# Attention: the causal mask inside the running product, and full steps' running product over pairs of keys

## The chip, the cores and the metric

The kernel runs on one core of a Trainium2 chip. The metric is the device time of one execution in microseconds (us), as the median of several runs. The engines are PE (matrix products; PEld is its loading of weights), DVE (vector), ACT (activation functions), POOL (general vector) and SP (issues DMAs). Each works through its own queue in order; semaphores order them among each other.

## The reference

One decoder block on a sequence of 2048 tokens with 1024 channels, all in float32. What matters here is the attention with 8 heads of 64 channels:

```python
def stick_breaking_attention(q, k, v):
    for i in range(S // Q_BLOCK):                      # 128 queries at a time
        L = (i + 1) * Q_BLOCK
        ...
        z = jnp.einsum('bhqd,bhkd->bhqk', qb, kb) * inv_sqrt
        mask = s_idx < t_idx                           # strictly causal
        log1m = jnp.where(mask, -jax.nn.softplus(z), 0.0)
        after = lax.cumsum(log1m, axis=3, reverse=True) - log1m
        logw = jax.nn.log_sigmoid(z) + after
        w = jnp.where(mask, jnp.exp(jnp.where(mask, logw, 0.0)), 0.0)
        outs.append(jnp.einsum('bhqk,bhkd->bhqd', w, vb))
```

Written without logarithms, the weight of key s for query t is sigmoid(z[t,s]) times the product of sigmoid(-z[t,j]) over all keys j with s < j < t. The block also has an input projection, a pooling mixer, an output projection, two normalizations with modulation, and a gated feed-forward part.

## The kernel before

The kernel has three parts in time. First come the modulation vectors and the first projections. Then comes the **attention stage**, in which the rest of the projections and some of the pooling run as fillers between the attention's steps. Last comes the output projection with the feed-forward part. Within the first two parts the order on PE, ACT, DVE and POOL is the order in which the program issues its instructions (a manual schedule), so every engine's queue follows the loop that is described here.

The attention loops over heads `h`, over blocks of 512 queries `tb`, and over blocks of 512 keys `sc`, from `sc = tb` down to 0. Such a triple is a *unit*, and it has four *steps* `i` of 128 queries each. Units with `sc == tb` lie on the diagonal (`diag`): their step `i` covers only the first `L = (i + 1) * 128` keys. All other units have full steps with `L = 512`. There are 128 diagonal steps and 192 full ones.

One step goes through the engines as follows; the lines are those of the kernel before.

- `weights_step`, on PE: two score products into `z` (L835, L836), and on the diagonal a third one (L838) that adds -1e30 to the masked keys by multiplying an identity with `neg_r`. On ACT: `sg`, the sigmoid of the scores (L840), and `pr`, the sigmoid of their negative (L842). A masked score gives `sg` 0 and `pr` 1.
- `scan_step`: DVE forms the running product of `pr` from the last key to the first, in place (L853). Its start is 1, or the `carry` that came from the unit with the later keys. Its second operand `idle` is not used (`ALU.bypass`); it lies in PSUM. POOL puts the start behind the last key (L850 on the diagonal, L852 elsewhere), takes the new `carry` out of key 0 (L857, except where `sc == 0`), and multiplies: `w[s] = sg[s] * pr[s + 1]` (L859).
- `turn_step`, seven steps later (`OFF = 7`): PE transposes the parts of `w` (L870). ACT and DVE split the result into a high part `wth` and a rest `wtl` (`split`, L60 and L61; the rest is `wt` from PSUM less `wth`).
- `values_step`, two steps after that: PE multiplies both with the values into `av` (L885, L886), and ACT copies `av` out at the end of a block of queries.

`scan_step` runs one step behind `weights_step`. `sg` has 5 buffers, `pr` has 6 and `w` has 11; `z` has two banks in the stage and the transposes have three. Beside this, POOL forms the rests of the projections' weights (`wq_l`, `wk_l`, `wu_l`, also L61) and the sums of the pooling windows (L392, L400) in the stage. Outside the stage, `u_a_l` and `wvl` (L61), `um` on DVE (L403) and POOL's products `s` (L1239) and sums (L1249) are instructions of the other parts that the prediction compares with.

Of the kernel before, what the change touches and what calls it, by code (L numbers as in the profile page):

```python
# [9 lines left out]
F32 = mybir.dt.float32  # L10
F32R = mybir.dt.float32r
AF = mybir.ActivationFunctionType
ALU = mybir.AluOpType
# [4 lines left out]
P = 128  # L18
# [10 lines left out]
TB = 512  # L29
NTB = S // TB  # L30
NT = S // P
EPS = 1e-6
NEG = -1e30
LAG = 2
OFF = 7
PRB = 6
# [9 lines left out]
def block_kernel(ctx, tc, x, c, w_cond, b_cond, g_mix_pre, g_mix_post, w_in, w_pool,  # L46
                 pool_scale, w_out, g_ffn_pre, g_ffn_post, w_gate, w_up, w_down, out):
    nc = tc.nc
# [25 lines left out]
    def open_pool(stack, name, bufs=1, side=None):  # L74
        kw = {"side": side} if side else {}
        return stack.enter_context(tc.tile_pool(name=name, bufs=bufs, reuse_waits="tile", **kw))
# [22 lines left out]
    ident = const.tile([P, P], F32, tag="ident", name="ident")  # L99
# [43 lines left out]
    c1 = open_pool(ph1, "c1")  # L143
# [3 lines left out]
    def psum(tag, bufs, name):  # L147
        return psp.tile([P, TB], F32, tag=tag, bufs=bufs, name=name)
# [7 lines left out]
    def bank_cycle(*tags):  # L156
        tags = itertools.cycle(tags)
        return lambda name: psum(next(tags), 1, name)

    z_ps, t_ps, av_ps, mm_only = bank_cycle("z0", "z1", "z2"), bank_cycle("w0", "w1"), bank_cycle("a0", "a1"), bank_cycle("mm")  # L160

    ident_r = c1.tile([P, P], F32R, tag="ident_r", name="ident_r")
    nc.vector.tensor_copy(ident_r, ident)
    ones = c1.tile([P, P], F32, tag="ones", name="ones")
    nc.vector.memset(ones, 1.0)
    one = ones[:, 0:1]
    ones_r = c1.tile([P, P], F32R, tag="ones_r", name="ones_r")
    nc.vector.tensor_copy(ones_r, ones)
    neg32 = c1.tile([P, P], F32, tag="neg32", name="neg32")
    nc.gpsimd.memset(neg32, 0.0)  # L170
    nc.gpsimd.affine_select(out=neg32, in_=neg32, compare_op=ALU.is_gt, fill=NEG, base=0,
                            pattern=[[-1, P]], channel_multiplier=1)
    neg_r = c1.tile([P, P], F32R, tag="neg_r", name="neg_r")
    nc.vector.tensor_copy(neg_r, neg32)
    rcnt = c1.tile([P, 16], F32, tag="rcnt", name="rcnt")
    for j in range(16):
        nc.gpsimd.memset(rcnt[:, j:j + 1], 1.0 / (j + 1))
# [249 lines left out]
    base = {"q": 0, "k": SBW, "u": 3 * SBW}  # L427
# [376 lines left out]
    att = open_pool(ph1, "att", bufs=2)  # L804
# [17 lines left out]
    qts, carries, avs, wss = {}, {}, {}, {}  # L822
# [3 lines left out]
    def weights_step(u, i):  # L826

        h, tb, sc = u
        diag = sc == tb
        kt, qt = kv[h, sc][0], qts[h, tb]  # L830
        L = (i + 1) * P if diag else TB
        nm = f"{h}_{tb}_{sc}_{i}"
        z = z_ps(f"z{nm}")
        keys = kt[:, 0:L]
        nc.tensor.matmul(z[:, 0:L], qt[:, 0, i * P:(i + 1) * P], keys, start=True, stop=False)  # L835
        nc.tensor.matmul(z[:, 0:L], qt[:, 1, i * P:(i + 1) * P], keys, start=False, stop=not diag)  # L836
        if diag:
            nc.tensor.matmul(z[:, i * P:L], ident_r, neg_r, start=False, stop=True)  # L838
        sg = att.tile([P, TB], F32, tag="sg", bufs=5, name=f"sg{nm}")
        nc.scalar.activation(sg[:, 0:L], z[:, 0:L], AF.Sigmoid, scale=0.125)  # L840
        pr = att.tile([P, TB + 1], F32, tag="pr", bufs=PRB, name=f"pr{nm}")
        nc.scalar.activation(pr[:, 0:L], z[:, 0:L], AF.Sigmoid, scale=-0.125)  # L842
        scans.append((u, i, pr, sg, L, nm))

    def scan_step(u, i, pr, sg, L, nm):

        diag = u[1] == u[2]
        carry = carries.pop(i, None)
        if carry is None:
            nc.gpsimd.memset(pr[:, L:L + 1], 1.0)  # L850
        else:
            nc.gpsimd.tensor_copy(pr[:, L:L + 1], carry)  # L852
        nc.vector.tensor_tensor_scan(pr[:, 0:L][:, ::-1], pr[:, 0:L][:, ::-1], idle[:, 0:L],  # L853
                                     one if carry is None else carry, ALU.mult, ALU.bypass)
        if u[2]:
            carries[i] = att.tile([P, 1], F32, tag=f"carry{i}", bufs=2, name=f"carry{nm}")
            nc.gpsimd.tensor_copy(carries[i], pr[:, 0:1])  # L857
        w = att.tile([P, TB], F32, tag="w", bufs=OFF + 4, name=f"w{nm}")
        nc.gpsimd.tensor_tensor(w[:, 0:L], sg[:, 0:L], pr[:, 1:L + 1], ALU.mult)  # L859
        wss.setdefault(u, []).append(w)  # L860

    def turn_step(u, b):

# [41 lines left out]
    def fillers():  # L905
        yield from pieces(1, chunks, tasks, [first_filler])
        while urgent:
            urgent.pop(0)()
# [3 lines left out]
    fill = fillers()  # L912
# [9 lines left out]
        next(fill)  # L922
    taken = START
    attending = True
    idle = psum("z2", 1, "idle")
    nc.vector.memset(idle, 0.0)
    z_ps, t_ps, av_ps, mm_only = bank_cycle(*('z0', 'z1')), bank_cycle(*('w0', 'w1', 'a1')), bank_cycle(*('a0',)), bank_cycle(*('mm',))
    steps = [(u, i) for u in units for i in range(4)]

# [63 lines left out]
    for n in range(len(steps) + OFF):  # L993
# [4 lines left out]
        if n < len(steps):  # L998
            u, i = steps[n]
            if i == 0:  # L1000
                unit_loads(u)
            weights_step(u, i)
            spent += 2.5 if u[1] == u[2] else 4.0
        if len(scans) > 1 or n >= len(steps) and scans:
            scan_step(*scans.pop(0))
        if n >= OFF:
            u, b = steps[n - OFF]
# [4 lines left out]
        while fill is not None and taken < goal:  # L1012
            taken += 1
            if next(fill, 0) == 0:
                fill = None
# [708 lines left out]
```

## Time and profile before

| | |
|---|---|
| median of 3 runs | 2292.85 us (2292.36 to 2293.82) |
| profiled execution, first to last instruction (its span) | 2290.2 us |
| attention stage in it | about 306 to 836 us |
| PE / DVE / ACT / POOL busy over the span | 2256.1 / 1617.8 / 1164.4 / 1299.5 us |
| granted PE clock, mean over the span | 0.997 |

The profiled execution has no time of its own beside its span; the span is 2.65 us shorter than the median of the timed runs. Busy times are unions of the instructions' own times. A duration of an instruction is longer than its distance to the next one on its engine, because the next one starts before the last results are written. In a group's row, `x192 | 243.8, 1270` means 192 instructions that were busy for 243.8 us in all and took 1270 ns each; behind the second bar stands the idle time of the engine just before them, with what ended it. In a row of the form `a/b/c`, these are the shortest, the median and the longest duration in ns. In a timeline's row the first two numbers are start and duration in us.

### The profile page before, as it was taken

The page shows a single profiled execution, that of the slowest core. Times are in us where ns is not written, and L with a number is a line of the kernel's source. Part 1 is how long each engine was busy: PE and PEld are TensorE (multiplying, and loading weights), DVE is VectorE, ACT ScalarE, POOL GpSimd, SP SyncE. Part 2 cuts the span into 40 slices and gives each one's busy share as a digit, 9 for nine tenths or more (in the row PEclk, how much of TensorE's full clock was granted, in tenths as well). Part 3 has the DMA queues.
Part 4 walks back from the last instruction along what each step waited for, and adds up shares of the span by engine and source line. Part 5 has one row for each costly group of instructions (what it writes and reads, how often), then busy time and mean ns, then how long its engine had stood idle before and what let it go on. Part 6 is the DMA issues. An engine that isn't in the chain of part 4 may idle for free.

```text
span 2290.2 us, 33477 instructions
## 1 busy us (share of the span) xinstructions
PE 2256.1 (99%) x10733; PEld 1858.6 (81%) x10733; DVE 1617.8 (71%) x2212; ACT 1164.4 (51%) x2418; POOL 1299.5 (57%) x1609
## 2 busy tenths in 40 slices
PE   7999999999999999999999999999999999999998
PEld 5878888888888878887888888888888888888887
DVE  6874569999999967657656555786766565555566
ACT  4334568998999855444232322555533323234444
POOL 3552257877878865555777778331486665651003
PEclk9999999999999999999999999999999999999999
DMA  8885763443333556665545455876753333328654
GB/s 294 304 277 197 282 175 106 125 120 103 100 105 100 170 175 224 216 227 166 163 155 165 152 166 171 281 239 212 251 187 111 106 111 97 111 89 293 213 187 147
DMA packets 312973, 405.18 MB, mean 177 GB/s; under 512 B 19863, under 2 KB 180187, under 8 KB 312669
## 3 DMA queue, kind: packets, MB, share of 16 engines
q1 hardware_dynamic: 308476, 400.68, 54.2%
q10 hardware_dynamic: 4320, 2.36, 0.4%
q8 instruction: 85, 1.39, 0.3%
q14 instruction: 92, 0.75, 0.1%
HBM read 274.51 MB, written 128.45 MB: 176 GB/s over the span
## 4 chain that ended last, share of the span: by engine, by line
PE 87%; DVE 7%; ACT 2%; POOL 2%; DMA 1%; issue 1%; SPq 0%; DVEq 0%; POOLq 0%; ACTq 0%
PE wt L870 4%; PE t_g L70 3%; PE t_g L71 3%; PE t_u L71 3%; PE t_u L70 3%; PE t_u L72 3%; PE t_g L72 3%; DVE pr L853 3%; PE dn0p L71 3%; PE dn0p L72 3%; PE dn0p L70 3%; PE dn1p L71 3%; PE dn1p L70 3%; PE dn1p L72 3%; PE b_u L71 3%; PE b_g L71 3%
## 5 line engine op out<-in xcount | busy, mean ns | idle before, releaser
L859 POOL TENSOR_TENSOR w<-sg,pr 128x512 f32<-128x512 f32 (+2 forms) x320 | 307.2, 960 | 44.5 <-DVE pr L853 30.7
L1239 POOL TENSOR_TENSOR s<-s,cu 128x512 f32<-128x512 f32 x88 | 131.8, 1504 | 237.8 <-DVE cu L1238 154.3
L853 DVE TENSOR_TENSOR_SCAN pr<-pr,carry,idle 128x512 f32<-128x512 f32 x192 | 243.8, 1270 | 0.0
L840 ACT ACTIVATE sg<-z 128x512 f32<-128x512 f32 (+2 forms) x320 | 183.4, 573 | 50.2 <-PE z L838 30.3
L61 DVE TENSOR_TENSOR wtl<-wt,wth 128x512 fp32r<-128x512 f32 (+1 forms) x320 | 188.4, 589 | 18.9 <-ACT wth L60 17.7
L60 ACT CAST wth<-wt 128x512 fp32r<-128x512 f32 (+1 forms) x320 | 182.3, 571 | 12.1 <-PE wt L870 12.1
L842 ACT ACTIVATE pr<-z 128x512 f32<-128x512 f32 (+2 forms) x320 | 182.6, 571 | 0.0
L870 PE MATMUL wt<-ident,w 128*128 128x128 f32 x1088 | 172.6, 273 | 0.9 <-POOL pr L850 0.7
L61 DVE TENSOR_TENSOR u_s_l<-u_s,u_s_h 128x512 fp32r<-128x512 f32 x66 | 64.7, 980 | 146.3 <-ACT u_s_h L60 146.3
L870 PEld LDWEIGHTS wt<-ident,w 128*128 128x128 f32 x1088 | 128.8, 141 | 27.7 <-POOL pr L850 1.2
L1229 ACT ACTIVATE s<-s 128x512 f32<-128x512 f32 x88 | 55.7, 632 | 183.3 <-DVE s L1228 183.3
L885 PE MATMUL av<-wth,vt 128*128 128x512 f32 (+1 forms) x320 | 128.1, 400 | 0.3 <-ACT o L890 0.2
L61 DVE TENSOR_TENSOR u_a_l<-u,u_a_h 128x512 fp32r<-128x512 f32 x66 | 74.2, 1125 | 69.9 <-ACT u_a_h L60 69.9
L835 PE MATMUL z<-kt,qt 128*128 128x512 f32 (+2 forms) x320 | 119.1, 372 | 3.5 <-DMA qt<-qd 2.0
L886 PE MATMUL av<-wtl,vt 128*128 128x512 f32 (+1 forms) x320 | 118.8, 371 | 2.9 <-DVE wtl L61 2.5
L71 PE MATMUL dn0p<-w0p_l,g0p_h 128*128 128x512 f32 x308 | 120.8, 392 | 0.6 <-DVE w0p_l L61 0.6
L70 PE MATMUL dn0p<-w0p_h,g0p_h 128*128 128x512 f32 x308 | 120.5, 391 | 0.0
L72 PE MATMUL dn0p<-w0p_h,g0p_l 128*128 128x512 f32 x308 | 120.3, 391 | 0.0
L836 PE MATMUL z<-kt,qt 128*128 128x512 f32 (+2 forms) x320 | 116.8, 365 | 0.0
L71 PE MATMUL dn1p<-w1p_l,g1p_h 128*128 128x512 f32 x292 | 114.4, 392 | 0.0
L60 ACT CAST g_s_h<-g_s 128x512 fp32r<-128x512 f32 x66 | 39.6, 620 | 147.0 <-POOL g_s L1171 81.7
L70 PE MATMUL dn1p<-w1p_h,g1p_h 128*128 128x512 f32 x292 | 114.2, 391 | 0.0
(696 smaller groups left out, 7188.5 us busy)
## 6 DMA issues: line engine op xcount, KB each, us to landing
g<-in_w_gate_dram SPq DMA_DIRECT2D x42, 512.0 KB, 5.3
u<-in_w_up_dram SPq DMA_DIRECT2D x42, 512.0 KB, 4.0
wc<-in_w_cond_dram SPq DMA_DIRECT2D x32, 512.0 KB, 7.0
qt<-qd SPq DMA_DIRECT2D x64, 256.0 KB, 3.9
wd<-in_w_down_dram SPq DMA_DIRECT2D x44, 256.0 KB, 3.5
tdt<-wd SPq DMA_DIRECT2D x44, 256.0 KB, 2.0
w0p<-tdt SPq DMA_DIRECT2D x44, 256.0 KB, 3.5
w1p<-tdt SPq DMA_DIRECT2D x44, 256.0 KB, 2.9
```

What stands on the lines that cost most here:

```text
L60: nc.scalar.copy(hi, src)
L61: low.tensor_tensor(lo, src, raw(hi), ALU.subtract)
L70: nc.tensor.matmul(ps, lh, rh, start=first and i == 0, stop=False)
L71: nc.tensor.matmul(ps, lh, rl, start=False, stop=False)
L72: nc.tensor.matmul(ps, ll, rh, start=False, stop=last and i == n - 1)
L840: nc.scalar.activation(sg[:, 0:L], z[:, 0:L], AF.Sigmoid, scale=0.125)
L842: nc.scalar.activation(pr[:, 0:L], z[:, 0:L], AF.Sigmoid, scale=-0.125)
L853: nc.vector.tensor_tensor_scan(pr[:, 0:L][:, ::-1], pr[:, 0:L][:, ::-1], idle[:, 0:L], one if carry is None else carry, ALU.mult, ALU.bypass)
L859: nc.gpsimd.tensor_tensor(w[:, 0:L], sg[:, 0:L], pr[:, 1:L + 1], ALU.mult)
L870: nc.tensor.transpose(wt[:, i * P:(i + 1) * P], wss[u][i][:, b * P:(b + 1) * P], ident)
L885: nc.tensor.matmul(av[:, lo0:], vb, wh[:, lo0:], start=first, stop=False)
L1239: nc.gpsimd.tensor_tensor(s, s, u, ALU.mult)
```

## The change

The mask's product on PE (L838) and its constants go. The mask is put into the running product of the diagonal steps: `begin`, in the PSUM bank that held `idle`, is zero with an identity in its last 128 columns, the product starts at zero and is `state * pr + begin`, so that it stays zero for the keys after the query, becomes 1 at the query's own key and is the product from there on. `w` then is zero at masked keys whatever `sg` is.

In full steps the running product goes over pairs. With `odd` and `even` as the two halves of `pr`, DVE forms `ends[m] = ends[m + 1] * odd[m] * even[m]` for 256 pairs, and one more DVE instruction multiplies the even elements of `sg` by `odd`. POOL then multiplies each pair of `sg` by the same `ends[m + 1]`, which is read twice through a repeated access. POOL's copy of the start goes to the end of `ends`, and the carry is taken from `ends[0]`. On each engine the order of the other instructions stays.

```diff
-        nc.tensor.matmul(z[:, 0:L], qt[:, 1, i * P:(i + 1) * P], keys, start=False, stop=not diag)
-        if diag:
-            nc.tensor.matmul(z[:, i * P:L], ident_r, neg_r, start=False, stop=True)
+        nc.tensor.matmul(z[:, 0:L], qt[:, 1, i * P:(i + 1) * P], keys, start=False, stop=True)
...
+    def keep_carry(u, i, left, nm):
+        if u[2]:
+            carries[i] = att.tile([P, 1], F32, tag=f"carry{i}", bufs=2, name=f"carry{nm}")
+            nc.gpsimd.tensor_copy(carries[i], left)
+
     def scan_step(u, i, pr, sg, L, nm):
+
         diag = u[1] == u[2]
         carry = carries.pop(i, None)
-        if carry is None:
-            nc.gpsimd.memset(pr[:, L:L + 1], 1.0)
+        w = att.tile([P, TB], F32, tag="w", bufs=OFF + 4, name=f"w{nm}")
+        wss.setdefault(u, []).append(w)
+        if diag:
+            keys = pr[:, 0:L][:, ::-1]
+            nc.gpsimd.memset(pr[:, L:L + 1], 0.0)
+            nc.vector.tensor_tensor_scan(keys, keys, begin[:, TB - L:][:, ::-1], zero, ALU.mult, ALU.add)
+            keep_carry(u, i, pr[:, 0:1], nm)
+            nc.gpsimd.tensor_tensor(w[:, 0:L], sg[:, 0:L], pr[:, 1:L + 1], ALU.mult)
         else:
-            nc.gpsimd.tensor_copy(pr[:, L:L + 1], carry)
-        nc.vector.tensor_tensor_scan(pr[:, 0:L][:, ::-1], pr[:, 0:L][:, ::-1], idle[:, 0:L],
-                                     one if carry is None else carry, ALU.mult, ALU.bypass)
-        if u[2]:
-            carries[i] = att.tile([P, 1], F32, tag=f"carry{i}", bufs=2, name=f"carry{nm}")
-            nc.gpsimd.tensor_copy(carries[i], pr[:, 0:1])
-        w = att.tile([P, TB], F32, tag="w", bufs=OFF + 4, name=f"w{nm}")
-        nc.gpsimd.tensor_tensor(w[:, 0:L], sg[:, 0:L], pr[:, 1:L + 1], ALU.mult)
-        wss.setdefault(u, []).append(w)
+            even, odd = (pr[:, 0:TB].rearrange("p (m two) -> p m two", two=2)[:, :, n] for n in range(2))
+            sg2 = sg.rearrange("p (m two) -> p m two", two=2)
+            ends = att.tile([P, TB // 2 + 1], F32, tag="ends", bufs=4, name=f"ends{nm}")
+            nc.gpsimd.tensor_copy(ends[:, TB // 2:], carry)
+            nc.vector.tensor_tensor_scan(ends[:, 0:TB // 2][:, ::-1], odd[:, ::-1], even[:, ::-1], carry, ALU.mult, ALU.mult)
+            nc.vector.tensor_tensor(sg2[:, :, 0], sg2[:, :, 0], odd, ALU.mult)
+            keep_carry(u, i, ends[:, 0:1], nm)
+            nc.gpsimd.tensor_tensor(w.rearrange("p (m two) -> p m two", two=2), sg2,
+                                    ends[:, 1:].unsqueeze(2).broadcast_to([P, TB // 2, 2]), ALU.mult)
...
-    idle = psum("z2", 1, "idle")
-    nc.vector.memset(idle, 0.0)
+    begin = psum("z2", 1, "begin")
+    nc.vector.memset(begin, 0.0)
+    nc.vector.tensor_copy(begin[:, TB - P:], ident)
```

The constants `ident_r`, `neg32`, `neg_r` and `one` are no longer made; `zero` ([P, 1]) is new.

More of the change, by code (lines that the diff above doesn't have):

```diff
@@ L32 @@
 EPS = 1e-6
-NEG = -1e30
 LAG = 2
@@ L160, in block_kernel @@
     z_ps, t_ps, av_ps, mm_only = bank_cycle("z0", "z1", "z2"), bank_cycle("w0", "w1"), bank_cycle("a0", "a1"), bank_cycle("mm")
-    ident_r = c1.tile([P, P], F32R, tag="ident_r", name="ident_r")
-    nc.vector.tensor_copy(ident_r, ident)
     ones = c1.tile([P, P], F32, tag="ones", name="ones")
     nc.vector.memset(ones, 1.0)
-    one = ones[:, 0:1]
     ones_r = c1.tile([P, P], F32R, tag="ones_r", name="ones_r")
     nc.vector.tensor_copy(ones_r, ones)
[L169 to L174, printed above, removed]
+    zero = c1.tile([P, 1], F32, tag="zero", name="zero")
+    nc.vector.memset(zero, 0.0)
     rcnt = c1.tile([P, 16], F32, tag="rcnt", name="rcnt")
```

## The prediction

> **What bounds the kernel now.** I read the page's busy shares first, then the busy time by stage, then the chain of waits inside the stage that the change touches, then the groups of instructions by shape, and last the timeline of single instructions. The page says that PE is busy all the time, and the stage row (306 to 836 us is the attention stage, from the first to the last score matmul and what drains behind it) says that there it is not alone:
>
> ```profile
> PE 2256.1 (99%) x10733; PEld 1858.6 (81%) x10733; DVE 1617.8 (71%) x2212; ACT 1164.4 (51%) x2418; POOL 1299.5 (57%) x1609
> ...
> core 0: us, PE busy (x) PEld busy (x) DVE busy (x) ACT busy (x) POOL busy (x), PEclk, DMA share, GB/s
> ...
> 306.00:836.00 530.00, 522.22 (x3036) 440.67 (x3035) 508.51 (x658) 468.25 (x1066) 421.81 (x912) 1.00 0.42 120
> ```
>
> DVE is busy for 508.5 of 530 us, POOL for 421.8. The chain of waits by line, for the whole stage, gives DVE's running products (`pr`, L853) and residues (`wtl`, L61) 14.6% + 7.2% = 21.8%, some 116 us; the rest is mostly PE. So PE and DVE take turns at the end of the chain, and work moved onto either shows at once.
>
> ```profile
> by line: PE wt L870 16.0%; DVE pr L853 14.6%; PE av L886 9.3%; PE z L836 8.6%; PE z L835 8.6%; PE av L885 8.5%; DVE wtl L61 7.2%; PE u L70 2.7%; PE u L71 2.7%; PE u L72 2.7%; issue 1.7%; PE k L70 1.7%; PE k L71 1.6%; PE k L72 1.6%; DMA qt<-
> ```
>
> A step is one product on DVE: 192 full ones (512 keys) and 128 on the diagonal.
>
> ```profile
> L853 DVE TENSOR_TENSOR_SCAN pr<-pr,carry,idle x192: 1261/1270/1276, 317.3 to 821.2; 128x512 f32<-128x512 f32 x192
> L853 DVE TENSOR_TENSOR_SCAN pr<-pr,ones,idle x128: 455/864/1273, 309.3 to 797.6; 128x128 f32<-128x128 f32 x32, 128x256 f32<-128x256 f32 x32, 128x384 f32<-128x384 f32 x32, 128x512 f32<-128x512 f32 x32
> ```
>
> Adding up from each product's start to the next one's in the timeline (320 of them, first at 309.3, last at 821.2, so 511.9 us), the full steps take 330.5 us, **1.72 each**, and the diagonal ones 181.4, 1.42 each. Where DVE sets the pace a full step is 1.19 (479.00 to 480.19) + 0.58 (480.19 to 480.77) = 1.77:
>
> ```profile
> 479.00 1.27 DVE L853 TENSOR_TENSOR_SCAN pr<-pr,carry,idle 128x512 f32<-128x512 f32 x1
> 480.19 0.66 DVE L61 TENSOR_TENSOR wtl<-wt,wth 128x512 fp32r<-128x512 f32 x1
> 480.77 0.68 DVE L61 TENSOR_TENSOR q<-q,q 128x512 fp32r<-128x512 f32 x1
> ...
> 480.40 0.18 POOL L857 COPY carry<-pr 128x1 f32<-128x1 f32 x1 [0.41 <-DVE pr L853]
> 480.53 1.10 POOL L859 TENSOR_TENSOR w<-sg,pr 128x512 f32<-128x512 f32 x1
> ```
>
> POOL's `w` (480.53 to 481.63) lies beside DVE's next instructions, and none of these gets longer. That is the point on which the forecast rests: today's product reads `pr` from SBUF and `idle` from PSUM, and `wtl` reads `wt` from PSUM, one SBUF tensor each. DVE instructions that read two SBUF tensors behave otherwise. In the next fence, the durations (min/median/max) are of `wtl`, and then of two such tensor products and one scalar-tensor-tensor; below them stand one blocked instruction and POOL's around it:
>
> ```profile
> L61 DVE TENSOR_TENSOR wtl<-wt,wth x320: 259/664/695, 315.1 to 836.1; 128x512 fp32r<-128x512 f32 x128, 128x256 fp32r<-128x256 f32 x32
> ...
> L61 DVE TENSOR_TENSOR u_a_l<-u,u_a_h x66: 673/1262/1780, 1017.5 to 2054.7; 128x512 fp32r<-128x512 f32 x66
> ...
> L61 DVE TENSOR_TENSOR wvl<-spare,wvh x16: 410/416/961, 167.6 to 186.3; 128x256 fp32r<-128x256 f32 x16
> ...
> L403 DVE SCALAR_TENSOR_TENSOR um<-us,u x8: 671/692/1267, 88.3 to 168.7; 128x512 f32<-128x512 f32 x8
> ...
> 1408.39 1.05 DVE L61 TENSOR_TENSOR u_a_l<-u,u_a_h 128x512 fp32r<-128x512 f32 x1 [1.44 <-ACT u_a_h L60]
> ...
> 1407.58 1.30 POOL L1249 TENSOR_TENSOR gs<-s,s 128x512 f32<-128x512 f32 x1
> 1408.96 1.62 POOL L1249 TENSOR_TENSOR s<-s,s 128x512 f32<-128x512 f32 x1
> ```
>
> `wtl` never exceeds 695 ns. `u_a_l`, as large, takes 673 when alone and up to 1780. The single case shows why: POOL's `gs` ends at 1408.88, and `u_a_l`, issued at 1408.39, ends at 1409.44, 0.56 after that, so it waited for POOL and then did nearly its whole work (0.68 less 0.12). POOL's next then takes 1.62 instead of 1.30: it waits for DVE in turn. The two exclude each other for whole instructions.
>
> **The change, part by part.** *Pair product.* In a full step the scan covers 256 pairs instead of 512 keys, and DVE gets one product of 256 more (192 added instructions). Both read two SBUF tensors (`odd` and `even` of `pr`; `sg` and `odd`).
>
> ```profile
> L853 DVE TENSOR_TENSOR_SCAN pr<-pr,ones,idle 128x256 f32<-128x256 f32 x32 | 23.5, 735 | 0.0
> ...
> 499.23 0.74 DVE L853 TENSOR_TENSOR_SCAN pr<-pr,ones,idle 128x256 f32<-128x256 f32 x1
> 499.88 0.66 DVE L61 TENSOR_TENSOR wtl<-wt,wth 128x512 fp32r<-128x512 f32 x1
> ...
> L859 POOL TENSOR_TENSOR w<-sg,pr 128x512 f32<-128x512 f32 x224 | 245.7, 1097 | 32.0 <-DVE pr L853 19.5 <-ACT wth L60 3.4 <-DVE wtl L61 1.9
> ```
>
> A scan of 256 takes 0.735 (0.65 to the next start), and I take it for the pair scan: both count 256 results, with a second operation that was idle before. The product takes 0.41 as `wvl`, or 0.33 to the next start (less the 0.08 by which 0.66 and 0.58 of `wtl` differ). DVE alone would need 0.65 + 0.33 + 0.58 = 1.56 where it needed 1.77. But now scan, product and POOL's `w` exclude each other, and in one step they follow one another: `w` needs the product. Only `wtl` (0.58) fits beside `w`; the next scan is then issued and waits for `w` to end. From the end of one `w` to the end of the next: scan 0.735 - 0.12 = 0.61; product 0.33; hand-over to POOL 0.13 (479.00 + 1.27 = 480.27 to 480.40); `w` 1.10. That is **2.17**, and 192 x (2.17 - 1.72) = **+86 us**. The two one-element copies on POOL (0.19 each) fall beside the waits of this round: at nothing, or at most 0.12 x 192 = 23 if each held DVE up in full.
>
> The Trainium skill, page "SBUF — State Buffer", section "Who interferes with whom", states this as a rule: a Vector instruction with two SBUF inputs contends with a GpSimd instruction that reads SBUF, and the later one blocks for the whole of the other. The rows above agree for three shapes; no row here shows a scan with two SBUF inputs, which the rule would include.
>
> *POOL's `w`* reads one factor per pair, each twice, from `ends`. No row shows that pattern. The nearest rows for 512 elements are `w` itself, 1097, and products of other tiles at 1284 when alone:
>
> ```profile
> L1239 POOL TENSOR_TENSOR s<-s,cu x88: 1284/1604/1839, 1040.5 to 2072.4; 128x512 f32<-128x512 f32 x88
> ```
>
> At 1.29 a step costs 0.19 more, 36 us in all. Below, if the second factor were read only half as often, a quarter of the 0.9 us that the elements take would go: -0.23 x 192 = -44. I take +18, half-way to the dearer row, since the new operand runs at another pace than `sg` and no longer keeps today's fixed offset.
>
> [...]
>
> *POOL's other work in the stage* also reads SBUF and now adds to the round:
>
> ```profile
> L61 POOL TENSOR_TENSOR wu_l<-wu,wu_h 128x256 fp32r<-128x256 f32 x16 | 11.8, 739 | 0.0
> ...
> L400 POOL TENSOR_TENSOR um<-us,um 128x512 f32<-128x512 f32 x8 | 10.4, 1295 | 0.1
> ...
> L61 POOL TENSOR_TENSOR wk_l<-wk,wk_h 128x256 fp32r<-128x256 f32 x12 | 8.8, 737 | 0.0
> ...
> L392 POOL TENSOR_TENSOR us<-u 128x527 f32<-128x527 f32 x8 | 8.5, 1066 | 0.0
> ...
> L61 POOL TENSOR_TENSOR wq_l<-wq,wq_h 128x256 fp32r<-128x256 f32 x9 | 6.7, 740 | 0.0
> ```
>
> These are 46 us. If all that falls into full steps (some 0.7 of the stage) counted, +32; if POOL caught up in the diagonal steps, 0. A diagonal step lasts 1.42 and gives POOL about 0.95 (a `w` of 128 to 512 keys, a memset, a copy), so it leaves 0.45 x 128 = 58 us free. I take +10.
>
> *Diagonal steps.* Scan shapes stay, `begin` lies in PSUM as `idle` did, only the second operation is now an add instead of none: no change (the neighbours are the diagonal forms themselves). PE loses 128 mask matmuls, each 0.06 apart from the next:
>
> ```profile
> 322.47 0.22 PE L838 MATMUL z<-neg_r,ident_r 128*128 128x128 f32 x1
> 322.53 0.27 PE L870 MATMUL wt<-ident,w 128*128 128x128 f32 x1
> ```
>
> 128 x 0.06 = 8 us off PE. I count 0 (range 0 to -8): when full steps wait for DVE and POOL, PE has that time to spare. The dropped constants cost nothing, since what follows them waits for loads and statistics anyway (here DVE is idle for 3.10 us):
>
> ```profile
> 2.64 0.22 DVE L174 CAST neg_r<-neg 128x128 fp32r<-128x128 f32 x1
> ...
> 7.53 0.15 DVE L115 TENSOR_SCALAR x_v<-ss 128x1 f32<-128x1 f32 x1 [3.10 <-ACT xt L316]
> ```
>
> The one new copy into `begin` stands once, ahead of the stage, at some 0.2 us.
>
> *Who waits behind.* A late `w` holds the transposes (`wt`, PE) seven steps on, and through five `sg` buffers ACT, and through ACT the next scores; so the stage takes the round's pace within a few steps. DMAs keep their order and their consumers come later, so no load becomes late.
>
> Sum: 86 + 18 + 10 = **+114 us**. The profiled execution's span is 2290.2, 2.65 below the median of the three runs; the difference lies outside the span and stays. 2292.85 + 114 = **2407**.
>
> **The rivals.** *Nothing is blocked (faster).* If scan and product did not exclude POOL, DVE's round would be 1.56, and its 116 us on the chain are 116/1.77 = 65 steps' worth, 0.21 less each: -14, and up to -8 from PE; as PE takes over, about -16 in all: 2277. It decides as soon as a full step's DVE work fits beside `w`. For it: today's scans lie beside `w` untouched. Against it: every DVE shape here with two SBUF tensors was blocked.
>
> *Only the added product is blocked.* A scan yields an element only every 2.1 ns ((1270 - 735)/256), half the product's rate, and may leave POOL room. Then `wtl` and scan (1.23) cover `w` with its hand-over (1.23), the product rarely waits, DVE's 1.56 is below PE's pace, and waits and gains cancel: 2287 to 2293, about no change.
>
> *The pair scan costs more.* Two live multiplications in the feedback might cost a pair what two keys cost today, 1.27: +0.535 x 192 = +103 on top, about 2510. Against it: nothing but the row of the one-operation form speaks for 0.735.
>
> **How the numbers follow.** Blocking of scan and product: 0.86. Nothing blocked: 0.06. Only the product: 0.05. Dearer scan: 0.03. Within the first case the low end has `w` at its cheap bound, 86 - 44 + 10 = +52 and a little more for hand-overs, 2350; the high end has 86 + 36 + 32 and half the copies, +165, 2460. That range leaves out about 0.04 of the first case, so it holds 0.82 and need not reach the others. A measurement tells 0.2% (4.6 us) from no change: faster 0.07, same 0.05, slower 0.88.
>
> **What would show it.** Right: in the profile after, the pair scan's median is well over 0.735 or its start is at the end of a `w`, the product or `w` is longer than 0.41 and 1.10 in many cases, full steps take 2.1 to 2.45, PE's idle time in the stage grows by about 100 us, diagonal steps stay near 1.4, and what follows the stage only moves later. Wrong: scans overlap `w` at 0.735 and 1.10 each (a rival has it), or the scan takes 1.27 with no POOL instruction beside it.

## The result, and the profile after

| | before | after |
|---|---|---|
| median of 4 runs (lowest to highest) | 2292.78 us (2292.36 to 2293.82) | 2383.86 us (2383.35 to 2384.76) |
| time / time before, 95% interval | | 1.0400 (1.0387 to 1.0412) |
| span of the profiled execution | 2290.2 us | 2382.3 us (+92.1) |
| first to last running product (attention stage) | 511.9 us | 605.4 us |
| a full step (192) | 1.72 us | 2.215 us |
| a diagonal step (128) | 1.42 us | 1.41 us |

The changed kernel is 91 us slower. The lines of the page of after that answer to those shown of before, busy time first, then the chain of waits by engine over the whole span:

```profile
PE 2280.2 (96%) x10605; PEld 1851.0 (78%) x10605; DVE 1716.0 (72%) x2404; ACT 1170.4 (49%) x2418; POOL 1398.3 (59%) x1607
...
PE 72%; DVE 21%; ACT 2%; POOL 2%; DMA 2%; issue 1%; SPq 0%; DVEq 0%; POOLq 0%; ACTq 0%
```

PE lost 128 matmuls, DVE gained 192 instructions, and both are busy for longer. Where that happens, the busy time by stretch of after says, here for the attention stage and for what follows it.

```profile
core 0: us, PE busy (x) PEld busy (x) DVE busy (x) ACT busy (x) POOL busy (x), PEclk, DMA share, GB/s
...
306.00:927.00 621.00, 545.09 (x2898) 432.50 (x2897) 604.20 (x850) 474.00 (x1065) 523.56 (x910) 0.98 0.36 102
927.00:2382.30 1455.30, 1445.00 (x6397) 1188.30 (x6395) 927.96 (x1273) 567.17 (x1088) 759.36 (x551) 1.00 0.55 178
```

The stage lasts 621 us where it lasted 530. What follows takes 1455.3 us, against 1454.2 (2290.2 less 836), so it only starts later. In the stage DVE is now busy for 604.2 of 621 us (97%) and PE stands idle for 621 - 545.1 = 75.9 us, against 7.8. The chain of waits of after, for the stage alone, shows the same change of hands:

```profile
by line: DVE ends L858 31.6%; DVE wtl L60 20.7%; DVE sg L859 14.8%; DVE pr L850 8.4%; PE wt L872 3.4%; PE av L888 2.2%; issue 2.0%; PE z L828 1.7%; PE z L827 1.6%; ACT pr L832 1.5%; PE av L887 1.4%; ACT wth L59 1.3%; POOL w L861 0.8%; DVE k
```

Before, two lines of DVE had 21.8% of this chain; now four have 75.5%. The durations of these instructions in after (smallest/median/largest in ns, then where the first and the last start):

```profile
L858 DVE TENSOR_TENSOR_SCAN ends<-pr,carry x192: 732/1286/1635, 316.2 to 913.6; 128x256 f32<-128x256 f32 x192
...
L859 DVE TENSOR_TENSOR sg<-sg,pr x192: 390/396/1453, 317.5 to 914.8; 128x256 f32<-128x256 f32 x192
...
L861 POOL TENSOR_TENSOR w<-sg,ends x192: 1084/1090/1574, 318.1 to 916.5; 128x512 f32<-128x512 f32 x192
...
L850 DVE TENSOR_TENSOR_SCAN pr<-pr,zero,begin x128: 451/862/1274, 308.2 to 885.9; 128x128 f32<-128x128 f32 x32, 128x256 f32<-128x256 f32 x32, 128x384 f32<-128x384 f32 x32, 128x512 f32<-128x512 f32 x32
...
L60 DVE TENSOR_TENSOR wtl<-wt,wth x320: 257/662/694, 313.8 to 928.1; 128x512 fp32r<-128x512 f32 x128, 128x256 fp32r<-128x256 f32 x32
```

The pair scan can take 732 ns, and takes 1286 in the median: longer than the 1270 in which it did 512 keys before. `wtl` and the diagonal scans, which have an operand in PSUM, are as long as they were. One round of the timeline of after (start, duration) shows why. POOL's rows stand below DVE's:

```profile
561.11 1.29 DVE L858 TENSOR_TENSOR_SCAN ends<-pr,carry 128x256 f32<-128x256 f32 x1
562.32 0.40 DVE L859 TENSOR_TENSOR sg<-sg,pr 128x256 f32<-128x256 f32 x1
562.63 0.68 DVE L60 TENSOR_TENSOR wtl<-wt,wth 128x512 fp32r<-128x512 f32 x1
563.23 1.29 DVE L858 TENSOR_TENSOR_SCAN ends<-pr,carry 128x256 f32<-128x256 f32 x1
...
560.75 1.09 POOL L861 TENSOR_TENSOR w<-sg,ends 128x512 f32<-128x512 f32 x1
561.79 0.58 POOL L857 COPY ends<-carry 128x1 f32<-128x1 f32 x1
562.45 0.30 POOL L838 COPY carry<-ends 128x1 f32<-128x1 f32 x1
562.88 1.09 POOL L861 TENSOR_TENSOR w<-sg,ends 128x512 f32<-128x512 f32 x1
```

The scan is issued at 561.11, while `w` runs until 561.84, and ends at 562.40, 0.56 after it: it waited, and then did nearly its whole work. It is no single case: of the 192 pair scans of after, 162 take longer than 743 ns, each of them was issued while a POOL instruction ran, and each ends 0.54 to 0.55 us (unrounded) after the end of that instruction; the other 30 take 732 to 743. The product follows, `w` starts 0.16 after the product's end, and beside `w` there is room for `wtl` alone; the next scan, at 563.23, waits again until 563.97. From one scan to the next this is 2.12 us. POOL's copy of one element, 0.18 before, lasts 0.58, which is also the median of these copies here: it waits for the scan in turn.

### The profile page after: what moved, and what is told of

It is laid out like the page before. It is cut to its first block, busy times and chain, and to the rows that moved or that the text cites. A ratio compares the mean times of both kernels' runs of the same rounds, so it can differ in the third digit from the quotient of the medians.

```text
span 2382.3 us, 33187 instructions
## 1 busy us (share of the span) xinstructions
PE 2280.2 (96%) x10605; PEld 1851.0 (78%) x10605; DVE 1716.0 (72%) x2404; ACT 1170.4 (49%) x2418; POOL 1398.3 (59%) x1607
## 4 chain that ended last, share of the span: by engine, by line
PE 72%; DVE 21%; ACT 2%; POOL 2%; DMA 2%; issue 1%; SPq 0%; DVEq 0%; POOLq 0%; ACTq 0%
DVE ends L858 8%; DVE wtl L60 5%; DVE sg L859 4%; PE t_g L69 3%; PE t_g L70 3%; PE t_u L70 3%; PE t_u L69 3%; PE t_u L71 3%; PE t_g L71 3%; PE dn0p L70 3%; PE dn0p L69 3%; PE dn0p L71 3%; PE dn1p L70 3%; PE dn1p L69 3%; PE dn1p L71 3%; PE b_u L70 2%
## 5 line engine op out<-in xcount | busy, mean ns | idle before, releaser
L861 POOL TENSOR_TENSOR w<-sg,ends 128x512 f32<-128x512 f32 x192 | 220.5, 1148 | 39.3 <-DVE sg L859 18.4
L830 ACT ACTIVATE sg<-z 128x512 f32<-128x512 f32 (+2 forms) x320 | 178.3, 557 | 126.5 <-PE z L828 115.5
L858 DVE TENSOR_TENSOR_SCAN ends<-pr,carry 128x256 f32<-128x256 f32 x192 | 235.1, 1224 | 0.0
L872 PE MATMUL wt<-ident,w 128*128 128x128 f32 x1088 | 177.7, 278 | 16.7 <-POOL w L861 8.4
L59 ACT CAST wth<-wt 128x512 fp32r<-128x512 f32 (+1 forms) x320 | 176.5, 552 | 19.4 <-PE wt L872 19.2
L888 PE MATMUL av<-wtl,vt 128*128 128x512 f32 (+1 forms) x320 | 128.6, 402 | 52.5 <-DVE wtl L60 52.0
L872 PEld LDWEIGHTS wt<-ident,w 128*128 128x128 f32 x1088 | 136.9, 142 | 53.3 <-DVE wtl L60 11.7
L832 ACT ACTIVATE pr<-z 128x512 f32<-128x512 f32 (+2 forms) x320 | 177.1, 554 | 0.0
L888 PEld LDWEIGHTS av<-wtl,vt 128*128 128x128 f32 x320 | 61.5, 192 | 90.3 <-DVE wtl L60 84.9
L859 DVE TENSOR_TENSOR sg<-sg,pr 128x256 f32<-128x256 f32 x192 | 117.9, 614 | 0.0
```

The lines of the kernel that those rows point to most:

```text
L59: nc.scalar.copy(hi, src)
L858: nc.vector.tensor_tensor_scan(ends[:, 0:TB // 2][:, ::-1], odd[:, ::-1], even[:, ::-1], carry, ALU.mult, ALU.mult)
L859: nc.vector.tensor_tensor(sg2[:, :, 0], sg2[:, :, 0], odd, ALU.mult)
L861: nc.gpsimd.tensor_tensor(w.rearrange("p (m two) -> p m two", two=2), sg2, ends[:, 1:].unsqueeze(2).broadcast_to([P, TB // 2, 2]), ALU.mult)
L872: nc.tensor.transpose(wt[:, i * P:(i + 1) * P], wss[u][i][:, b * P:(b + 1) * P], ident)
L888: nc.tensor.matmul(av[:, lo0:], vb, wl[:, lo0:], start=False, stop=last)
```

## The experiments

Two theories were set against each other from the start. **E**, the exclusion: a DVE instruction that reads two tensors from SBUF and a POOL instruction that reads SBUF never run at the same time, so scan, product and `w` stand in one row. **S**, dearer work: the pair scan costs more because it multiplies twice, or because of the strides or of the added instruction itself. Rows of the runs below name lines of their own kernels. The runs e5, e1, e2 and e3 ran beside the kernel before at 2290.86 us; e6, e7, e8 and e9 beside it at 2291.39; e4 and e10 beside it at 2290.46. A full step is counted as in the prediction, from scan start to scan start, over 192.

### The old kernel with the exclusion added (e5_idle_sbuf)

```diff
 # the kernel before
-        nc.vector.tensor_tensor_scan(pr[:, 0:L][:, ::-1], pr[:, 0:L][:, ::-1], idle[:, 0:L],
+        nc.vector.tensor_tensor_scan(pr[:, 0:L][:, ::-1], pr[:, 0:L][:, ::-1], (idle if diag else still)[:, 0:L],
...
+    still = att.tile([P, TB], F32, tag="still", bufs=1, name="still")
+    nc.vector.memset(still, 0.0)
```

> The kernel before, with the unused operand of the full steps' running product in SBUF instead of PSUM (diagonal steps keep it in PSUM; nothing else changes, no pairs, no strides). Theory E (a DVE instruction with two SBUF tensors and a POOL instruction that reads SBUF exclude each other): a full step becomes scan 1.27 - 0.12, hand-over 0.13, w 1.10 = 2.38 us instead of 1.72, so 192 x 0.66 = +127, about 2420 us, scans up to 2.3 us long. Rival S (the pair scan is dear by its strides or its second multiplication): no change, 2293 us, all full scans at 1.27.

Measured: 2422.38 us, 1.0576 (1.0561 to 1.0592). The full steps' scan, which took 1261 to 1276 ns before:

```profile
L853 DVE TENSOR_TENSOR_SCAN pr<-pr,carry,still x192: 1266/1728/2360, 317.1 to 944.2; 128x512 f32<-128x512 f32 x192
```

The arithmetic is untouched and the second operation ignores this operand; only its address has moved from PSUM to SBUF. That alone costs 132 us. The shortest scans are as short as before, and the 163 that take over 1.3 us each end 1.08 us after the POOL instruction that ran when they were issued. The exclusion therefore holds for scans, and it is enough that the operand lies in SBUF. The sum came out as expected (127), its split did not: a full step takes 2.22 us instead of the expected 2.38, and a diagonal one, whose operands stayed where they were, 1.63 instead of 1.42. How a wait moves from full steps into the diagonal ones was not separated.

### The change with one or both instructions freed (e1_scan_psum, e2_prod_psum, e3_both_psum)

Each of these reads a constant in PSUM in place of one operand: e1 leaves the even factors out of the running product, e2 leaves the odd ones out of the weights, e3 does both.

```diff
 # e1 and e3
-            nc.vector.tensor_tensor_scan(ends[:, 0:TB // 2][:, ::-1], odd[:, ::-1], even[:, ::-1], carry, ALU.mult, ALU.mult)
+            nc.vector.tensor_tensor_scan(ends[:, 0:TB // 2][:, ::-1], odd[:, ::-1], begin[:, 0:TB // 2], carry, ALU.mult, ALU.mult)
 # e2 and e3
-            nc.vector.tensor_tensor(sg2[:, :, 0], sg2[:, :, 0], odd, ALU.mult)
+            nc.vector.tensor_tensor(sg2[:, :, 0], sg2[:, :, 0], begin[:, 0:TB // 2], ALU.mult)
```

The scan alone freed:

> The changed kernel, with the pair scan's second factor read from a constant in PSUM (the even factors are left out of the running product). E: the scan is no longer blocked, 0.735 us each; the product still is, but scan and wtl (1.23) cover w with its hand-over (1.23), so full steps take about 1.65 to 1.75 and the time is 2280 to 2300. S by strides or by two multiplications: the other factor is still strided and both multiplications are still made, so the scan stays near 1.2 and the time near 2384.

Measured: 2298.79 us, 1.0035 (1.0023 to 1.0047); a full step 1.72 us. The rows of e1:

```profile
L858 DVE TENSOR_TENSOR_SCAN ends<-pr,carry,begin x192: 727/733/742, 317.7 to 827.7; 128x256 f32<-128x256 f32 x192
...
L859 DVE TENSOR_TENSOR sg<-sg,pr x192: 390/403/1323, 318.4 to 828.4; 128x256 f32<-128x256 f32 x192
```

With both multiplications live the scan takes 733 ns in every case, so the dearer arithmetic of S is out (the constant is zero here; with real factors, in e9 below, it is 740). The product is still blocked: 83 of the 192 take longer than 433 ns, up to 1323.

The product alone freed:

> The changed kernel, with the added product's second factor read from a constant in PSUM (the odd factors are left out of it). E: the product takes 0.40 always and can run beside POOL, but the scan is still blocked by w, and w still follows the product: a full step of 2.0 us instead of 2.2, some 2340 us (2320 to 2370); scans keep a median over 1.2. Rival P (only the added product is blocked, and scans wait for something else): 2293 or less. S: 2384, unless the product itself was slowed.

Measured: 2337.35 us, 1.0205 (1.0188 to 1.0222); a full step 1.89 us. The time is E's, the scan's median is not:

```profile
L858 DVE TENSOR_TENSOR_SCAN ends<-pr,carry x192: 733/996/1750, 316.5 to 860.8; 128x256 f32<-128x256 f32 x192
...
L859 DVE TENSOR_TENSOR sg<-sg,begin x192: 386/391/406, 317.8 to 862.4; 128x256 f32<-128x256 f32 x192
```

The timeline of e2 shows what the expectation overlooked:

```profile
501.26 0.87 DVE L858 TENSOR_TENSOR_SCAN ends<-pr,carry 128x256 f32<-128x256 f32 x1
...
500.48 1.10 POOL L861 TENSOR_TENSOR w<-sg,ends 128x512 f32<-128x512 f32 x1
...
501.52 0.59 POOL L857 COPY ends<-carry 128x1 f32<-128x1 f32 x1
...
502.04 0.18 POOL L838 COPY carry<-ends 128x1 f32<-128x1 f32 x1
...
502.19 1.09 POOL L861 TENSOR_TENSOR w<-sg,ends 128x512 f32<-128x512 f32 x1
```

With the product out of POOL's way, POOL goes from `w` to copy to copy to `w` without a gap, 1.71 us in this round (500.48 to 502.19). The scan still ends 0.55 after `w` (502.13 after 501.58), as in after, but by now it is issued later into `w`, so that its own length shows less of the wait. The length of a blocked instruction measures when it was issued; the end of what blocked it is what can be read.

Both freed:

> Both constants at once: scan and product each read one SBUF tensor (even factors left out of the scan, odd ones out of the product). E: no DVE instruction of a full step excludes POOL; scan 0.735, product 0.41, DVE's round is 1.56 and PE sets the pace: 2270 to 2285 us, below the kernel before. S: scans stay near 1.2 us, the time near 2384 or somewhat below.

Measured: 2283.03 us, 0.9967 (0.9955 to 0.9979), 101 us below the change; a full step 1.64 us. The rows of e3, and its chain of waits for the stage:

```profile
L858 DVE TENSOR_TENSOR_SCAN ends<-pr,carry,begin x192: 731/737/745, 314.4 to 809.7; 128x256 f32<-128x256 f32 x192
...
L859 DVE TENSOR_TENSOR sg<-sg,begin x192: 391/396/404, 315.0 to 810.3; 128x256 f32<-128x256 f32 x192
...
by line: PE wt L872 19.0%; PE av L888 10.4%; PE z L827 10.3%; PE z L828 10.2%; PE av L887 10.2%; issue 3.0%; DVE ends L858 2.5%; DVE wtl L60 2.5%; PE u L69 2.3%; PE u L71 2.3%; PE u L70 2.3%; PE q L69 2.1%; PE q L70 2.1%; PE q L71 2.1%; PE 
```

Every scan and product runs at its bare length, although 176 of the 192 scans were issued while a POOL instruction ran. DVE all but leaves the chain, and PE takes it over. All instructions of the change are there; only one operand of each is another one, in PSUM. The two operands together account for the whole loss. They do not add up: freeing the scan alone gives back 85 us, the product alone 47, both 101. Once one of the two is freed, less of the other's wait is left on the path: e1, with its 83 blocked products, is only 16 us above e3.

### The two halves of the change apart (e6_mask_only, e7_pairs_only)

e6 is the kernel before with the causal mask inside the product: `begin` in place of `idle`, an add in the diagonal scan, no mask matmul. e7 is the change with the mask back on PE:

```diff
 # e6, against the kernel before
-        if diag:
-            nc.tensor.matmul(z[:, i * P:L], ident_r, neg_r, start=False, stop=True)
...
+            nc.vector.tensor_tensor_scan(keys, keys, begin[:, TB - L:][:, ::-1], zero, ALU.mult, ALU.add)
 # e7, against the change
+        if diag:
+            nc.tensor.matmul(z[:, i * P:L], ident_r, neg_r, start=False, stop=True)
...
-            nc.vector.tensor_tensor_scan(keys, keys, begin[:, TB - L:][:, ::-1], zero, ALU.mult, ALU.add)
+            nc.vector.tensor_tensor_scan(pr[:, 0:L][:, ::-1], pr[:, 0:L][:, ::-1], idle[:, 0:L], one, ALU.mult, ALU.bypass)
```

> The mask's part alone: begin inside the diagonal steps' running product, no mask matmul on PE, and the full steps as in the kernel before. The prediction counted 0 to -8 us for it (128 matmuls of 0.06 us). Theory E: the diagonal scans keep their lengths (0.47, 0.73, 1.00, 1.27), PE loses 8 us of work, of which a part is on the path, as PE sets the pace for half of the stage: 2285 to 2293 us. Rival: the add in the feedback or the later start makes the diagonal scans longer: above 2293.

Measured: 2294.26 us, 1.0011 (1.0002 to 1.0020): no gain, and just outside what was expected, on the rival's side. The rival's cause is not there: the diagonal scans are as long as before (455/864/1273). The row of these scans in e6, and the chain of waits for its stage:

```profile
L850 DVE TENSOR_TENSOR_SCAN pr<-pr,zero,begin x128: 455/864/1273, 309.0 to 798.9; 128x128 f32<-128x128 f32 x32, 128x256 f32<-128x256 f32 x32, 128x384 f32<-128x384 f32 x32, 128x512 f32<-128x512 f32 x32
...
by line: DVE pr L855 21.9%; DVE wtl L60 13.6%; PE wt L868 10.1%; PE av L884 6.1%; PE z L827 5.7%; PE z L828 5.6%; DVE pr L850 5.6%; PE av L883 5.3%; issue 3.9%; PE u L69 2.4%; PE u L70 2.3%; PE u L71 2.3%; ACT wth L59 1.6%; ACT pr L832 1.5%
```

Three lines of DVE have 41% of it, where two had 21.8% before, so the chain passes through DVE for longer. Why nothing at all was left of the time taken off PE stays open.

> The pairs alone: full steps as in the changed kernel, the mask still a third matmul on PE. E: DVE and POOL set the pace, PE has time to spare, so the mask's 8 us of matmuls show in part at most: 2384 to 2390 us. Rival: the parts add up (8 us more than the changed kernel, 2392).

Measured: 2383.23 us, 1.0405 (1.0390 to 1.0419), within 0.7 us of the change and 0.8 under the expected range. So the pair product carries all of the loss, and the mask none.

### The strides (e8_halves)

```diff
-            even, odd = (pr[:, 0:TB].rearrange("p (m two) -> p m two", two=2)[:, :, n] for n in range(2))
+            even, odd = (pr[:, n * TB // 2:(n + 1) * TB // 2] for n in range(2))
...
-            nc.vector.tensor_tensor(sg2[:, :, 0], sg2[:, :, 0], odd, ALU.mult)
+            nc.vector.tensor_tensor(sg[:, 0:TB // 2], sg[:, 0:TB // 2], odd, ALU.mult)
```

> The changed kernel with the two halves of the keys (first 256, last 256, contiguous) in place of the even and the odd keys, for scan and product (so the pairs are the wrong ones); sizes and engines are the same. E: strides play no part, 2380 to 2388 us. Rival S (strides make scan or product dear): scans back near 0.735 or the product below 0.40, and 30 to 90 us less.

Measured: 2383.53 us, 1.0403 (1.0389 to 1.0417); the scan's median is 1284 ns, against 1286:

```profile
L858 DVE TENSOR_TENSOR_SCAN ends<-pr,carry x192: 732/1284/1637, 315.3 to 910.0; 128x256 f32<-128x256 f32 x192
```

Strides of the scan and the product play no part.

### The product left out (e4_no_product)

```diff
-            nc.vector.tensor_tensor(sg2[:, :, 0], sg2[:, :, 0], odd, ALU.mult)
```

> The changed kernel without the added product (the odd factors are left out of the even keys' weights); the pair scan still reads two SBUF tensors. E: the round is scan 0.61, hand-over 0.13, w 1.10 = 1.84 us instead of 2.17, so 192 x 0.33 = 63 us less than the changed kernel's 2384, about 2321. If the two only shared the engine's time without excluding POOL: DVE's round would be 1.23 and the time at or below the kernel before, 2293 or less.

Measured: 2316.18 us, 1.0110 (1.0095 to 1.0126), 68 us below the change. The scan is still blocked:

```profile
L858 DVE TENSOR_TENSOR_SCAN ends<-pr,carry x192: 734/1186/1751, 316.3 to 840.4; 128x256 f32<-128x256 f32 x192
```

Even without the added instruction, with half as many elements in the scan, the kernel is slower than before: a blocked short scan costs more than a free long one. As in e5 the sum fits and the split does not: a full step takes 1.73 us instead of 1.84, a diagonal one 1.56 instead of 1.41 in the change.

### Real factors with the odd ones in PSUM (e9_odd_in_psum, e10_odd_own_bank)

If the place of one operand is the whole loss, the true odd factors in PSUM should bring e3's time with real factors. In e9 ACT writes them over the scores, with a third score bank, `z2`, which had held `begin`; in e10 they have the bank `z2` to themselves, one half per parity of the query tile. Both have the mask back on PE.

```diff
 # e9
+            even, odd = (z.rearrange("p (m two) -> p m two", two=2)[:, :, n] for n in range(2))
+            nc.scalar.activation(pr[:, 0:TB // 2], even, AF.Sigmoid, scale=-0.125)
+            nc.scalar.activation(odd, odd, AF.Sigmoid, scale=-0.125)
 # e10
+        odd = od[:, i % 2 * TB // 2:(i % 2 + 1) * TB // 2]
...
+            for n, half in enumerate((pr[:, 0:TB // 2], odd)):
+                nc.scalar.activation(half, z.rearrange("p (m two) -> p m two", two=2)[:, :, n], AF.Sigmoid, scale=-0.125)
```

> The pairs with real factors, one of the two in PSUM: ACT writes the odd factors over the scores' bank and the even ones to SBUF (two half activations instead of one, about +0.05 us a step on ACT); scan and product then read one SBUF tensor each. The bank that held the scan's spare operand becomes a third score bank, since a score bank is now free only after the product; the mask stays on PE. E: scans 0.735 to 0.75, products 0.41, neither blocked; a full step of 1.65 to 1.8, 2280 to 2310 us, the longer hold of the score banks deciding where. S by two multiplications or strides: scans near 1.2 as before, 2350 or more.

Measured: 2315.85 us, 1.0113 (1.0099 to 1.0126). Scan and product run unblocked (medians 740 and 396 ns, largest 744 and 418), 68 us of the loss are back, and still the time missed the expectation by 6 us at its upper end. The waits of e9 in the stage (in total us, times, longest), of which the last two are new and the first was 16.6 us before:

```profile
DVE wtl L61 <- ACT wth L60: 60.9, 111, 3.4
...
PEld z L835 <- DVE sg L872: 18.9, 32, 1.4
...
PE z L835 <- DVE sg L872: 10.8, 18, 1.2
```

The first row alone shows no loss: in e3, which is faster than the kernel before, it is 40.7. The other two are PE waiting for the product, because the score bank is now held until the product has read it. e10 takes that away:

> The pairs with real factors again, the odd ones now in two halves of the PSUM bank that held the scan's spare operand, so that the score banks are free as early as in the kernel before; the diagonal scans read a single column of that bank as their spare operand, and the mask stays on PE. ACT makes two half activations for one, +0.05 us a step. E: scans 0.735, products 0.40, nothing blocked, PE sets the pace: full steps 1.64 to 1.70, diagonal ones 1.42 to 1.48, 2280 to 2292 us, at or a little below the kernel before. If the longer hold of the score banks was not what cost e9_odd_in_psum its 24 us, but the split activations: 2310 or more.

Measured: 2304.95 us, 1.0065 (1.0052 to 1.0077), between the two expectations. The rows of e10's waits:

```profile
DVE ends L871 <- ACT od L847: 24.4, 77, 0.7
...
DVE wtl L61 <- ACT wth L60: 13.5, 19, 2.3
DVE pr L863 <- ACT od L847: 12.4, 21, 1.3
...
ACT od L847 <- DVE sg L872: 10.8, 39, 1.1
```

Giving the odd factors a bank of their own brought back 10 of e9's 24 us over the kernel before; the waits of the score matmuls on the product are gone. In their place DVE waits for ACT, which writes each step's factors in two instructions, and ACT waits for the product to free half the bank. A full step takes 1.70 us, as expected, and a diagonal one 1.56, where 1.42 to 1.48 was expected: the miss lies in the diagonal steps. How the remaining 14 us split between the waits was not separated. No version with the real factors came below the kernel before.

## Why the prediction was right

The forecast was 2407 us (2350 to 2460) for the case that scan, product and `w` exclude each other; 2383.86 came out, for that reason. Step by step:

- **The two exclude each other for whole instructions.** Shown for the scan by e5, where one operand's place is the only edit, and for scan and product together by e3. The Trainium skill, page "SBUF — State Buffer", section "SBUF: two separate sides", has whichever of the two starts first hold the shared ports for its whole instruction while the other is blocked; the prediction had no row of a scan to set against this rule, and here the 162 scans that end 0.54 to 0.55 us after POOL's end agree. What the runs add is that the operand need not be used.
- **The round of 2.17.** A clean round is 2.12 (the median from one pair scan to the next is 2.13): 0.56 from the end of `w` to the end of the scan (0.61 was put down), the rest nearly as put down. At 192 rounds that is (2.12 - 1.72) x 192 = +77, where the prediction had +86.
- **POOL's copies at nothing.** The first one waits beside the scan (0.58), the second lies in the hand-over (0.30); `w` starts 0.16 us after the product's end in the round shown, with 0.13 forecast.
- **POOL's other work in the stage, +10.** All 192 full steps take 425.2 us (2.215 each), 94.7 more than before; less the 77 of clean rounds this leaves 18 for every other disturbance, by difference. One such case stands in the timeline of after:

```profile
529.07 1.29 DVE L858 TENSOR_TENSOR_SCAN ends<-pr,carry 128x256 f32<-128x256 f32 x1
...
529.76 1.11 POOL L60 TENSOR_TENSOR wk_l<-wk,wk_h 128x256 fp32r<-128x256 f32 x1
530.27 0.88 DVE L859 TENSOR_TENSOR sg<-sg,pr 128x256 f32<-128x256 f32 x1
530.82 0.38 POOL L857 COPY ends<-carry 128x1 f32<-128x1 f32 x1
```

  A residue of another projection gets in between scan and product, and the product waits for its end (0.88 instead of 0.40). So 86 + 10 = 96 stands against 94.7. That the sum fits so well is luck: the round was put 9 us too high and the rest 8 too low.
- **The rate of `w`, +18: the step that was mis-sized.** `w` takes 1084 ns at least and 1090 in the median, against 1097 before. A factor read twice costs nothing. The page "GPSIMD Engine Reference" of the Trainium skill, section 3.1, has about 2.6 cycles an element for two inputs, by which 512 elements at its 1.2 GHz take 1.11 us (an estimate, without any dispatch); the measured 1.09 is near it, and the 1.28 of the dearer row is not. This term is 18 of the 23 us by which the forecast was too high; it had been set half-way towards the dearer row, and no row showed that an operand at another pace costs anything.
- **Diagonal steps and mask matmuls at nothing.** The diagonal steps take 180.2 us in all, against 181.4. By e6 and e7, taking the mask off PE is worth +3 and about 0 us. The 8 us taken off PE brought nothing anywhere.
- **What follows only moves later.** 1455.3 against 1454.2 us.
- **PE idle for about 100 us more.** It was 68 more. PE's busy time went up by 23 us in spite of the 128 matmuls less; some of its matmuls are longer (the second `av` 402 ns in the mean, against 371, with medians of 394 and 393), and the clock column has 0.98 in place of 1.00. How much each gives was not separated.

The rivals' prices can be checked too. "Nothing is blocked" was put at 2277, and e3, which is that case, took 2283.0, some 8 us below the kernel before instead of 16: its full steps take 16.5 us less than before, its diagonal ones 7.8 more. "Only the product is blocked" was put at 2287 to 2293, and e1 took 2298.8, 6 us above that range: waits and gains nearly cancel there, but a small loss is left. "The pair scan costs more" is out by the 733 ns of e1.

## What to carry to other kernels

Before work on DVE is halved by giving it two tensors, look where these tensors lie and what POOL does meanwhile: here a scan or a product with one operand in PSUM ran beside POOL, while one with both in SBUF took turns with POOL's instructions that read SBUF. What takes turns adds up: the round was scan, product and `w` in a row, not the longer of DVE's and POOL's shares. An operand that nothing uses counted as well, so a dummy one belongs in PSUM. To find such a case in a trace, compare smallest and median durations of one shape (732 and 1286 ns here) and look whether the long ones end a fixed time after an instruction of the other engine.

## What the runs showed of the hardware that was not expected

- A scan whose second operation ignores its operand is blocked all the same when this operand lies in SBUF: 1728 ns in the median against 1270, and 132 us for the kernel (e5).
- A scan with two live multiplications is as fast as one with a single one: 733 ns for 256 elements (e1), 740 with real factors (e9), against 735. A step of two elements in both inputs changes nothing (e8).
- A POOL copy of one element waits as a long instruction does: the copy of the start takes 0.58 us in the median of after, against 0.18 in e3.
- POOL reads an operand in which each element comes twice at the same pace as a plain one: 1090 ns for 512 elements, against 1097.
